# The loads of the Fourier position tables, issued behind the pooling windows instead of behind the values

## The chip, the cores and the metric

The kernel runs on one core of one Trainium2 chip. The metric is the time of one execution on the device, in microseconds (us). Before the change the median of three runs is 1839.31 us (1837.73 to 1840.53).

## What is computed

The reference is a two-layer encoder trunk over 512 positions of 1024 channels, in float32. Each layer adds half a SwiGLU feed-forward (inner width 2816), then a mixer, then half a second SwiGLU. The mixer projects the normalised input once and runs three groups beside each other:

```python
h = rmsnorm(x, mix_norm[l])
p = h @ w_in[l]                       # columns: a 256, f 256, q 512, k 512, v 512
y_pool = pool_mixer(a, pool_w[l], pool_scale[l])          # windows 2, 4, 8, 16, minus the token
y_four = fourier_mixer(f, fourier_w[l])                   # Re(2-D DFT over positions, channels) @ w
y_attn = diff_attention(q, k, v, lam, lam_init, head_norm)  # 4 heads, two softmaxes each
x = x + concatenate([y_pool, y_four, y_attn]) @ w_out[l]
```

The Fourier part along the positions is a product with tables of cosines and sines, which lie in memory (`dft_s`) and are loaded in each layer.

## The kernel before

All products are split into high and low parts: an operand is rounded to a high part on ScalarE (ACT), and the rest becomes the low part on VectorE (DVE), GpSimd (POOL), or through ACT and an accumulating DMA that POOL issues (`split`, L102; `produce`, L171). Three matmuls on TensorE (PE) then make one product (`mm3`, L106). Weights come in tiles of 128 x 1024 through a ring of 7 `st` buffers; SP issues their loads in a fixed sequence (`load`, L159). An operand is converted three ahead of its use (`AHEAD`).

Between these, the tiles of a layer's mixer come from one general pool of 54 buffers (`NG`, L52, `gen`, L77): inputs of the projections, scores, transposed scores, values, tables. PSUM has 8 banks.

The mixer (L605) is written as steps, and the string `ORDER` (L54) names them in the program's order; a scheduler then lays out each engine's instructions, gives out buffers as they come free, and places the waits. Each engine works through its own queue in order. The steps that matter here are:

- `V0`, `V1`, `VE`: the values, and their copy out of PSUM (vh, vl). `GD` loads fw and cs, the tables of the Fourier channels. `TD` (L816) loads the five tables of the positions, `tab`, into five buffers of the general pool, from ACT's queue. `TB` (L821) splits them, much later, for `FD0` and `FD1`.
- `T0` to `T3` transpose the scores of a head (L665): PE writes banks, ACT makes th, DVE tl. `X0` to `X3` weight the values by them (AV, then osq, osh, osl; L677). `Y0` to `Y3` normalise (ss, L274; L688).
- `S20` and the like are scores of a head and a block of queries (L637); `P3`, `A` and `F` are projections (pp, L614): head 3's queries and keys, the pooling input, the Fourier input.
- `GH` (L800) joins the channel tables with the Fourier weights: ACT and DVE split fw and cs, PE makes twelve matmuls, ACT and DVE split the result.
- `AE0`, `AE1` (L740) make the windows of the pooling on DVE (pad, win, m). `PD`, `PL0` and `PL1` (L734, L767) multiply them by the pooling weights: ACT and DVE split m, PE makes PL.
- `W0a` to `W3` are the output projection (wo, L863).

```python
def do_table_loads():
    four["rt"] = [g(w=NT, name="tab") for _ in range(5)]
    for j, t in enumerate(four["rt"]):
        nc.scalar.dma_start(t, dft_s[:, j * NT : (j + 1) * NT])
...
for n in ORDER:
    steps[n]()
```

Loads that SP and ACT issue count on eight semaphores in turn. Each load waits in its engine's queue until the load that had its semaphore before, eight loads earlier in the program, has landed.

Of the kernel before, what the change touches and what calls it, by code (L numbers as in the profile page):

```python
# [36 lines left out]
L = 2  # L37
# [14 lines left out]
NG = 54  # L52
NWARM = 8
ORDER = (  # L54
    "P0 N L P1 E1 P2 E0 S01 S11 S13 E2 V0 S03 S00 S10 S12 S22 S02 S21 T0 V1 GD VE TD T1 X0 S23 S20 Y0 P3 "
    "T2 PD X1 E3 Y1 A GH S30 S32 AE0 AE1 F PL0 X2 S31 S33 PL1 FE0 T3 W0a FE1 Y2 FG0 W1a FG1 TB X3 FD1 FD0 "
    "Y3 W0b W1b W2 W3"
).split()

C_FFN1, C_MIX, C_FFN2, C_FIN = 0, 16, 32, 48  # L60
# [941 lines left out]
```

## Time and profile before

| | us |
|---|---|
| median of three runs | 1839.31 |
| the profiled execution, whole | 1840.45 |
| its span, first to last instruction | 1838.7 |
| TensorE busy in the span | 1773.4 |
| VectorE busy | 1278.8 |
| ScalarE busy | 884.9 |

Times in the views are microseconds from the span's start. A row of the timeline has the start, the duration, the engine, the line of the kernel, the operation and the tiles written and read; in brackets is the idle time of the engine ahead of it and what ended that. `PEld` is the loading of a matmul's stationary operand, and ACTq, SPq and the like are the issuing of DMAs from an engine's queue. The granted clock is TensorE's, as a share of full speed.

### The profile page before, as it was taken

How to read it: one execution, taken by the hardware profiler on the slowest of the kernel's cores; microseconds unless marked ns; L12 is line 12 of the kernel's file. 1: busy time of each engine (PE TensorE's matmuls, PEld its weight loads, DVE VectorE, ACT ScalarE, POOL GpSimd, SP SyncE). 2: the span in 40 equal slices, each digit the busy share in tenths (PEclk: the TensorE clock that was granted, in tenths of full speed). 3: DMA queues.
4: the chain of work that ended last, by engine and by line, in shares of the span. 5: the costliest groups of instructions: out<-in, count | busy, mean ns of one | idle time of the engine just before them, and what ended most of it. 6: DMA issues, size and time to landing. Idle time of an engine off the chain costs nothing.

```text
span 1838.7 us, 28135 instructions
## 1 busy us (share of the span) xinstructions
PE 1773.4 (96%) x11286; PEld 1602.7 (87%) x11286; DVE 1278.8 (70%) x2004; ACT 884.9 (48%) x1223; POOL 204.8 (11%) x242
## 2 busy tenths in 40 slices
PE   8999999999899999999999999999988999999997
PEld 7889989877678989989899899998766899899895
DVE  7765846868679765847887477477776887477474
ACT  7433424468646533424554244244875554244243
POOL 1101001001101101001010010100111110010101
PEclk9999999999899999999999999999998999999998
DMA  7757757545625857857677586665444467586661
GB/s 240 184 149 161 197 133 175 143 124 131 138 67 130 192 160 154 202 130 179 152 169 188 136 195 173 138 169 155 115 118 104 102 158 188 133 200 162 140 158 46
DMA packets 81778, 279.69 MB, mean 152 GB/s; under 512 B 9200, under 2 KB 12784, under 8 KB 81648
## 3 DMA queue, kind: packets, MB, share of 16 engines
q0 software_dynamic: 29376, 106.97, 33.6%
q1 hardware_dynamic: 48528, 166.73, 28.0%
q10 hardware_dynamic: 3744, 4.21, 0.8%
q8 instruction: 88, 1.44, 0.3%
q14 instruction: 42, 0.34, 0.1%
HBM read 258.99 MB, written 2.10 MB: 142 GB/s over the span
## 4 chain that ended last, share of the span: by engine, by line
PE 79%; DVE 6%; ACT 5%; DMA 4%; issue 4%; POOL 1%; SPq 0%; ACTq 0%; DVEq 0%; POOLq 0%
PE dn L107 8%; PE dn L108 8%; PE dn L109 8%; PE qg L462 4%; PE qg L464 4%; PE qg L463 4%; PE qe L463 4%; PE qe L464 4%; PE qe L462 4%; PE qa L464 4%; PE qa L463 4%; PE qa L462 4%; DMA st<-in_gu 4%; PE qb L463 2%; PE qb L464 2%
## 5 line engine op out<-in xcount | busy, mean ns | idle before, releaser
L103 ACT ACTIVATE hi<-st 128x1024 fp32r<-128x1024 f32 (+2 forms) x420 | 432.9, 1035 | 621.4 <-PE dn L108 223.6
L104 DVE TENSOR_TENSOR lo<-st,hi 128x1024 fp32r<-128x1024 f32 (+2 forms) x420 | 500.7, 1194 | 194.5 <-ACT hi L103 193.0
L108 PE MATMUL dn<-al,hi 128*128 128x512 f32 x704 | 274.6, 390 | 0.0
L109 PE MATMUL dn<-ah,lo 128*128 128x512 f32 x704 | 274.2, 389 | 0.0
L107 PE MATMUL dn<-ah,hi 128*128 128x512 f32 x704 | 271.9, 392 | 0.5
L462 PE MATMUL qg<-xh,hi 128*128 128x256 f32 x688 | 196.9, 286 | 6.1 <-ACT hi L103 3.2
L462 PE MATMUL qe<-xh,hi 128*128 128x256 f32 x688 | 196.9, 286 | 4.3 <-DVE nv L328 2.3
L463 PE MATMUL qg<-xh,lo 128*128 128x256 f32 x688 | 196.1, 285 | 0.9 <-DVE lo L104 0.9
L464 PE MATMUL qg<-xl,hi 128*128 128x256 f32 x688 | 196.1, 285 | 0.0
L464 PE MATMUL qe<-xl,hi 128*128 128x256 f32 x688 | 195.6, 284 | 0.1
L463 PE MATMUL qe<-xh,lo 128*128 128x256 f32 x688 | 195.4, 284 | 0.0
L190 POOL DMA_DIRECT2D st<-in_gu x129 | 116.1, 901 | 673.1 <-DVE lo L104 600.3
L600 DVE SCALAR_TENSOR_TENSOR x<-dn,x 128x512 f32<-128x512 f32 x96 | 66.2, 690 | 168.6 <-PE dn L109 168.6
L107 PEld LDWEIGHTS dn<-ah,hi 128*128 128x128 f32 x704 | 131.3, 188 | 31.9 <-ACT ah L103 5.9
L108 PEld LDWEIGHTS dn<-al,hi 128*128 128x128 f32 x704 | 132.2, 188 | 29.0 <-DVE al L104 2.4
L109 PEld LDWEIGHTS dn<-ah,lo 128*128 128x128 f32 x704 | 132.2, 188 | 26.9
L462 PEld LDWEIGHTS qg<-xh,hi 128*128 128x128 f32 x688 | 133.3, 194 | 7.4 <-ACT hi L103 3.4
L462 PEld LDWEIGHTS qe<-xh,hi 128*128 128x128 f32 x688 | 132.4, 192 | 8.1 <-ACT hi L103 4.9
L463 PEld LDWEIGHTS qg<-xh,lo 128*128 128x128 f32 x688 | 133.5, 194 | 1.1 <-DVE lo L104 1.1
L463 PEld LDWEIGHTS qe<-xh,lo 128*128 128x128 f32 x688 | 132.6, 193 | 1.3 <-issue 0.7
L464 PEld LDWEIGHTS qg<-xl,hi 128*128 128x128 f32 x688 | 133.4, 194 | 0.0
L464 PEld LDWEIGHTS qe<-xl,hi 128*128 128x128 f32 x688 | 132.6, 193 | 0.4 <-DVE xl L104 0.3
(274 smaller groups left out, 3923.3 us busy)
## 6 DMA issues: line engine op xcount, KB each, us to landing
st<-in_gu SPq DMA_DIRECT2D x175, 512.0 KB, 4.6
st<-in_gu POOLq DMA_DIRECT2D x172, 512.0 KB, 5.7
st<-in_dn SPq DMA_DIRECT2D x64, 512.0 KB, 4.2
lo<-st POOLq DMA_DIRECT2D x32, 512.0 KB, 5.0
st<-in_dn SPq DMA_DIRECT2D x32, 384.0 KB, 3.2
st<-in_qk SPq DMA_DIRECT2D x16, 512.0 KB, 3.7
st<-in_wo SPq DMA_DIRECT2D x16, 512.0 KB, 3.8
st<-in_wv SPq DMA_DIRECT2D x8, 512.0 KB, 4.9
```

The source lines that it names most:

```text
L103: A.activation(hi, src, AF.Copy)
L104: (lo_eng or V).tensor_tensor(lo, src, f(hi), SUB)
L107: T.matmul(o, lh, rh, start=start, stop=False)
L108: T.matmul(o, lh, rl, start=False, stop=False)
L109: T.matmul(o, ll, rh, start=False, stop=stop)
L190: G.dma_start(t[:, 0:w], then, accum_op=ADD)
L462: T.matmul(o, wh[:, s], xh, start=start and p == 0 and z == 0, stop=False, **k)
L463: T.matmul(o, wl[:, s], xh, start=False, stop=False, **k)
L464: T.matmul(o, wh[:, s], xl, start=False, stop=stop and p == NK - 1 and z == 1, **k)
L600: V.scalar_tensor_tensor(X[m], b, 0.5, X[m], MUL, ADD)
```

## The change

The step `TD` moves in `ORDER`: from behind `VE`, the copy of the values, to behind `AE0` and `AE1`, ahead of the Fourier projection `F`.

```diff
 ORDER = (
-    "P0 N L P1 E1 P2 E0 S01 S11 S13 E2 V0 S03 S00 S10 S12 S22 S02 S21 T0 V1 GD VE TD T1 X0 S23 S20 Y0 P3 "
-    "T2 PD X1 E3 Y1 A GH S30 S32 AE0 AE1 F PL0 X2 S31 S33 PL1 FE0 T3 W0a FE1 Y2 FG0 W1a FG1 TB X3 FD1 FD0 "
-    "Y3 W0b W1b W2 W3"
+    "P0 N L P1 E1 P2 E0 S01 S11 S13 E2 V0 S03 S00 S10 S12 S22 S02 S21 T0 V1 GD VE T1 X0 S23 S20 Y0 P3 "
+    "T2 PD X1 E3 Y1 A GH S30 S32 AE0 AE1 TD F PL0 X2 S31 S33 PL1 FE0 T3 W0a FE1 Y2 FG0 W1a FG1 TB X3 "
+    "FD1 FD0 Y3 W0b W1b W2 W3"
 ).split()
```

Both layers use it. The instructions are the same in number and kind; the scheduler lays some of them out otherwise, on PE, DVE and ACT. POOL and SP keep their sequences. Layer 0 is shown, and layer 1 moves alike. In brackets stand the semaphores that an instruction waits for: those of the engines, and those of loads that SP and ACT issue (DMAHW) or POOL (DMASW).

On ACT, behind the copy of the values (vh), before: the five loads of the tables stand ahead of the conversions of T1 (th).

```order
L728 ACTIVATE vh_4463<-v_4133,ny_3840 128x512
L819 DMA tab_4467<-in_dft_s 128x258 [waits DMAHW5_49]
L819 DMA tab_4468<-in_dft_s 128x258 [waits DMAHW6_49]
L819 DMA tab_4469<-in_dft_s 128x258 [waits DMAHW7_49]
L819 DMA tab_4470<-in_dft_s 128x258 [waits DMAHW0_49,DVE_49]
L819 DMA tab_4471<-in_dft_s 128x258 [waits DMAHW1_49]
L103 ACTIVATE th_4482<-T_440_4477 128x512 [waits PE_49]
```

And now, at the same place:

```order
L728 ACTIVATE vh_4463<-v_4133,ny_3840 128x512
L103 ACTIVATE th_4472<-T_435_4467 128x512 [waits PE_49]
L103 ACTIVATE th_4481<-T_438_4476 128x512 [waits PE_49]
L103 ACTIVATE th_4490<-T_441_4485 128x512 [waits DVE_49,PE_49]
L103 ACTIVATE th_4499<-T_444_4494 128x512 [waits DVE_49,PE_49]
L684 ACTIVATE osq_4516<-AV_447_4503 128x512 [waits PE_49]
```

The five issues and their waits are gone from here; the conversions follow the values at once.

On ACT ahead of the high part of the pooling's m (g from m), before: two conversions of a W1a weight (hi, lo) stand among the exponentials and scalings of head 3's scores (sc).

```order
L657 ACTIVATE sc_4866<-sc_4866,rc_4862 128x512 [waits DVE_49]
L652 ACTIVATE sc_4895,rs_4883<-sc_4895,nb_4882 128x512
L186 ACTIVATE hi_5150<-st_4765 128x1024 [waits PE_49]
L657 ACTIVATE sc_4888<-sc_4888,rc_4884 128x512 [waits DVE_49]
L187 ACTIVATE lo_5151<-hi_5150 128x1024 [waits DMASW1_49,PE_49,Activation_49]
L103 ACTIVATE g_5005<-m_4907 128x512 [waits DVE_49]
```

And now:

```order
L657 ACTIVATE sc_4856<-sc_4856,rc_4852 128x512 [waits DVE_49]
L652 ACTIVATE sc_4885,rs_4873<-sc_4885,nb_4872 128x512 [waits DVE_49]
L186 ACTIVATE hi_4950<-st_4594 128x1024 [waits DMAHW0_49,PE_49]
L657 ACTIVATE sc_4878<-sc_4878,rc_4874 128x512 [waits DVE_49]
L187 ACTIVATE lo_4951<-hi_4950 128x1024 [waits DMASW0_49,PE_49,Activation_49]
L819 DMA tab_4931<-in_dft_s 128x258
L819 DMA tab_4932<-in_dft_s 128x258
L819 DMA tab_4933<-in_dft_s 128x258 [waits DMAHW4_49]
L819 DMA tab_4934<-in_dft_s 128x258 [waits DMAHW5_49]
L819 DMA tab_4935<-in_dft_s 128x258
L103 ACTIVATE g_5005<-m_4897 128x512 [waits DVE_49]
L186 ACTIVATE hi_5150<-st_4755 128x1024 [waits DMAHW1_49,PE_49]
```

The five issues stand ahead of m's high part, and the pair for the second W1a weight, hi_5150, has moved behind it; the pair of the first, hi_4950, stands in its place and used to stand ahead of the exponentials.

On DVE around the channel tables, before: the low part of cs (g from cs) stands behind the pooling's pads and waits for PE.

```order
L104 TENSOR_TENSOR g_4830<-fw_4447,g_4829 128x512 [waits DMAHW2_49,Activation_49,Pool_49]
L746 TENSOR_TENSOR pad_4903<-pp_515_4779,r_3902 128x512 [waits PE_49]
L753 TENSOR_TENSOR win_4908<-pad_4903 128x527 [waits DVE_49]
L753 TENSOR_TENSOR win_4910<-win_4908 128x525 [waits DVE_49]
L746 TENSOR_TENSOR pad_4920<-pp_516_4780,r_3902 128x512 [waits PE_49]
L104 TENSOR_TENSOR g_4832<-cs_4448,g_4831 128x256 [waits PE_49,Activation_49]
L104 TENSOR_TENSOR g_4845<-GH_4837,g_4844 128x512 [waits DVE_49,Activation_49]
```

And now:

```order
L104 TENSOR_TENSOR g_4820<-fw_4447,g_4819 128x512 [waits DMAHW2_49,Activation_49]
L104 TENSOR_TENSOR g_4822<-cs_4448,g_4821 128x256 [waits DMAHW3_49,Activation_49]
L746 TENSOR_TENSOR pad_4893<-pp_510_4769,r_3902 128x512 [waits PE_49]
L753 TENSOR_TENSOR win_4898<-pad_4893 128x527 [waits DVE_49]
L753 TENSOR_TENSOR win_4900<-win_4898 128x525 [waits DVE_49]
L746 TENSOR_TENSOR pad_4910<-pp_511_4770,r_3902 128x512 [waits PE_49]
L104 TENSOR_TENSOR g_4835<-GH_4827,g_4834 128x512 [waits Activation_49]
```

The low part of cs has moved ahead of the pads, behind that of fw, and waits for its load and ACT instead of PE. On PE the twelve GH matmuls stand in one run now; before, eight of them stood behind the first 17 matmuls of `F`. Further on, on DVE, the first window of the second half moves behind the end of m's first half, and the two narrow L764 of the second half move ahead of the low part of m.

## The prediction

> **What bounds the kernel now.** I read the page first. TensorE (PE) is busy for 96% of the span and carries 79% of the chain that ended last, so only time in which PE stands still, or runs at a lower clock, can be won.
>
> ```profile
> span 1838.7 us, 28135 instructions
> PE 1773.4 (96%) x11286; PEld 1602.7 (87%) x11286; DVE 1278.8 (70%) x2004; ACT 884.9 (48%) x1223; POOL 204.8 (11%) x242
> PE 79%; DVE 6%; ACT 5%; DMA 4%; issue 4%; POOL 1%; SPq 0%; ACTq 0%; DVEq 0%; POOLq 0%
> ```
>
> Then the timeline of PE through layer 0's mixer, between the values and the output projection. The columns are start, duration, engine, line and operation; the bracket is idle time before the row and what ended it.
>
> ```profile
> 444.70 0.39 PE L644 MATMUL S<-kh,qs 128*128 128x512 f32 x1
> 448.25 0.50 PE L276 MATMUL ss<-osh,ones 128*128 128x512 f32 x1 [1.16 <-ACT osh L103]
> ...
> 480.14 0.39 PE L109 MATMUL pp<-xh,lo 128*128 128x512 f32 x1
> 481.75 0.39 PE L107 MATMUL GH<-g,g 128*128 128x256 f32 x1 [1.23 <-ACT g L103]
> ...
> 484.15 0.39 PE L107 MATMUL pp<-xh,hi 128*128 128x512 f32 x1
> 487.78 0.39 PE L108 MATMUL pp<-xl,hi 128*128 128x512 f32 x1
> 488.07 0.39 PE L109 MATMUL GH<-g,g 128*128 128x256 f32 x1
> 489.12 0.39 PE L109 MATMUL pp<-xh,lo 128*128 128x512 f32 x1
> 495.94 0.39 PE L109 MATMUL pp<-xh,lo 128*128 128x512 f32 x1
> 499.37 0.80 PE L107 MATMUL PL<-g,g 128*128 128x512 f32 x1 [3.04 <-ACT g L103]
> 502.84 0.80 PE L108 MATMUL PL<-g,g 128*128 128x512 f32 x1 [1.81 <-DVE g L104]
> 508.12 0.63 PE L644 MATMUL S<-kh,qs 128*128 128x512 f32 x1
> ```
>
> Four idle times stand here: 1.16, 1.23, 3.04 and 1.81 us. From 484.15 to 487.78 there are 16 steps of one 512-column matmul: 0.227 us each. The eight GH matmuls from 488.07 to 489.12 take 0.131 us each. Third, the windows view, for the clock.
>
> ```profile
> 440.00:464.70 24.70, 21.91 (x102) 17.28 (x102) 17.32 (x39) 17.77 (x33) 4.53 (x5) 1.00 0.60 149
> 464.70:468.10 3.40, 1.10 (x4) 0.70 (x5) 3.27 (x6) 3.21 (x6) 1.27 (x1) 1.00 0.88 196
> 468.10:471.50 3.40, 3.40 (x10) 2.66 (x9) 2.29 (x4) 3.33 (x6) 0.00 (x0) 0.50 0.46 149
> 498.80:509.00 10.20, 7.81 (x18) 5.70 (x19) 5.45 (x14) 1.75 (x5) 0.85 (x1) 0.50 0.77 190
> 1410.20:1413.60 3.40, 1.54 (x8) 1.01 (x8) 3.30 (x13) 3.18 (x10) 0.38 (x1) 1.00 0.00 0
> 1413.60:1417.00 3.40, 3.40 (x12) 2.99 (x13) 3.40 (x11) 1.25 (x2) 0.00 (x0) 0.50 0.00 0
> ```
>
> After the stretch and its length come PE's busy time, the other engines', the granted clock (after POOL), the DMA share and GB/s. Where PE was busy for 1.10 or 1.54 of 3.4 us, the next 3.4 us ran at clock 0.50; through 440.0 to 464.7, with the 1.16 us idle time in it, the clock stayed 1.00. So a long idle time is paid twice: behind the one at 499.37 the clock was 0.50 for 10.2 us. A halved stretch of busy PE loses 1.7 us.
>
> Last, the timelines of ScalarE (ACT) and VectorE (DVE), for who makes PE wait, with the piece of the chain of waits at 439.21.
>
> ```profile
> 439.21 5.37 DMA st<-in_wo
> ```
>
> ```profile
> 441.41 0.39 ACTq L819 DMA_DIRECT2D tab<-in_dft_s  x1
> 441.47 1.27 ACT L728 ACTIVATE vh<-v,ny 128x512 fp32r<-128x512 f32 x2
> 444.60 0.33 ACTq L819 DMA_DIRECT2D tab<-in_dft_s  x1
> 444.98 2.07 ACT L103 ACTIVATE th<-T 128x512 fp32r<-128x512 f32 x4 [2.24 <-PE AV L109]
> 446.90 0.63 ACT L684 ACTIVATE osq<-AV 128x512 f32<-128x512 f32 x1
> 447.56 0.63 ACT L103 ACTIVATE osh<-osq 128x512 fp32r<-128x512 f32 x1
> ...
> 480.34 1.06 ACT L186 ACTIVATE hi<-st 128x1024 fp32r<-128x1024 f32 x1 [1.73 <-PE pp L108]
> 481.61 1.04 ACT L187 ACTIVATE lo<-hi 128x1024 fp32r<-128x1024 f32 x1
> ```
>
> ```profile
> 487.59 0.43 DVE L104 TENSOR_TENSOR g<-cs,g 128x256 fp32r<-128x256 f32 x1 [4.63 <-PE pp L108]
> 489.47 1.29 DVE L104 TENSOR_TENSOR g<-GH,g 128x512 fp32r<-128x512 f32 x2 [1.45 <-ACT g L103]
> 502.09 0.69 DVE L104 TENSOR_TENSOR g<-m,g 128x512 fp32r<-128x512 f32 x1
> 502.70 0.24 DVE L764 TENSOR_TENSOR m<-m,pad 128x8 f32<-128x8 f32 x2
> ```
>
> The fifth table load stands in ACT's queue and is issued only at 444.60: in the program it waits for the semaphore that the weight load of 439.21 also counts on, and that load landed at 439.21 + 5.37 = 444.58. Behind it stand T1's four conversions, osq and osh. And DVE idles 4.63 us before the low part of cs: its buffer is freed only by a matmul of the Fourier projection F, because the 54 buffers of the general pool are all taken, five of them by the tables.
>
> **The change part by part.** The two layers move alike; layer 1's rows below stand 900.5 us later (1399.87 for 499.37).
>
> *The five issues leave the place behind the values.* ACT's conversions then start behind vh, at 442.74 instead of 444.98. PE's eight score matmuls run from 444.70 without the small gap for a bank, which T1's conversions free, and end at 444.70 + 8 x 0.227 = 446.5. The last AV0 matmul stands one step before 444.70, so osq and osh (0.63 each) are done by about 446.2. So ss goes at 446.5 instead of 448.25: 1.75 us. What is late next is osl on DVE; it follows tl, which follows th, and both move by about 2 us, so ss's second matmul does not wait. Everything up to 480 is a chain behind this and moves along. Bounds: 0, if another wait takes the place; 2.24, ACT's whole idle time.
>
> *Five buffers stay free until the pooling is done.* In the new order the low part of cs is second behind fw's on DVE and waits for its load and ACT alone, and ACT converts cs ahead of the weight of L186. So GH starts behind the pooling projection A, at 480.14 + 0.23 = 480.37 instead of 481.75, and all twelve matmuls go together: 12 x 0.131 = 1.6; then 8 scores, 1.8; then F's 48 matmuls, 10.9: F ends at 494.7 instead of 495.94 + 0.23 = 496.2. That is 1.5 us.
>
> Behind F, PE waits for DVE. ACT does the L186 and L187 pair from 480.34 (1.06 and 1.04, end 482.5), then GH's high part (0.6, as osh): GH's low part starts on DVE at 483.1 instead of 489.47, 6.4 us earlier. From there to the low part of m (502.09) DVE has the same operations as before; the order puts two narrow L764 ahead of it, 0.2. So it starts at 502.09 - 6.4 + 0.2 = 495.9 and ends at 496.6. PE has one PL and three AV matmuls ahead of that wait (0.9, to 495.6), idles 1.0 us instead of 3.04 + 1.81, and does the eleven left in 2.5 us if the clock stays up: the next scores start at 499.1 instead of 508.12, **9.0 us**, the 1.5 included. One idle time of 1.0 us leaves a stretch of 3.4 us busy for 2.4, and 1.16 us did not lower the clock, so I take 1.00; the bounds are no wait at all (1.0 more) and one to two halved stretches (1.7 to 3.4 less).
>
> ```profile
> 1399.87 0.76 PE L107 MATMUL PL<-g,g 128*128 128x512 f32 x1 [3.04 <-ACT g L103]
> 1407.76 0.39 PE L644 MATMUL S<-kh,qs 128*128 128x512 f32 x1
> ```
>
> Layer 1 was halved for less long: 499.1 + 900.5 = 1399.6 instead of 1407.76, **8.2 us**.
>
> *The issues in their new place.* They stand on ACT between the conversion of the first W1a weight and m's high part: 5 x 0.39 = 2.0 us. Two of them still wait for a semaphore in the program, those of the next two wo loads behind that of 439.21; the second of these was issued 30 us earlier.
>
> ```profile
> 461.82 6.94 SPq L165 DMA_DIRECT2D st<-in_wo  x2
> ```
>
> F's first weight is free after 24 of F's 48 matmuls, 5.4 us before F ends; behind that ACT has 1.06, a scaling of about 0.7 and 1.04, then the issues: 4.8 us. So m's high part (0.6) is done about when F ends, and well before the low part that PE waits for anyway. I cost it at nothing; uncovered it would be up to 2.0 a layer. One weight pair moves behind m's high part; it belongs to W1b, the last but two of the projection's steps. SP and POOL keep their order.
>
> *The loads themselves.*
>
> ```profile
> DMA to landing us min/median/max: 4.9/5.7/8.0
> 532.89 1.65 ACT L103 ACTIVATE g<-tab 128x258 fp32r<-128x258 f32 x5
> ```
>
> Issued by about 493 and landed 8.0 later at worst, 501, against a use at 532.9 - 9.0 = 523.9 on the same scale: 23 us of cover.
>
> The Trainium skill's page "DMA: Bandwidth & Descriptors", section "Rules for kernel authors", speaks against the change: to overlap, issue a load early and wait for it late. Its section "Issuing engines are not separate DMA queues" adds that where a load is issued from saves only the issue time. By these the most to be had is those five issues' 2.0 us a layer, about 1836; the rows at 444.60 and 487.59 show two costs of an early issue that these sections leave out, so I do not follow them.
>
> **Sum.** 2 x 1.75 + 9.0 + 8.2 = 20.7 us. The profiled execution took 1840.45 us (span 1838.7 and 1.75 around it), so 1819.75 on its terms; the median of the three runs, 1839.31, stands 1.14 lower, which gives **1818.6**.
>
> **The rivals.**
> - *Half clock stays (0.14).* The wait for m's low part falls into a stretch that PE uses for less than about half, as at 464.70 and 1410.20, and each layer pays one or two halved stretches: 1822 to 1825. For: the stretches at 0.50 begin 3.4 us or multiples of it apart, and where they fall is chance. Against: 1.0 us is below the 1.16 that went free. On this the skill's "TensorE: Matmul & The Clock Gate", Part 1, is milder: half rate after at least one idle window of about 3.4 us. By that rule neither 1.0 nor 3.04 us halves the clock; the row at 498.80 shows that 3.04 did, so the measurement decides.
> - *Only the issue stall goes (0.06).* The pool stays full through other tiles, and cs waits as before: 2 x 1.75, so 1835.8. Against: the new order names no PE release for cs.
> - *Given back at the second FFN (0.06).* PE gets there 10 us earlier, but its first loads do not:
>
> ```profile
> 501.29 2.96 SPq L165 DMA_DIRECT2D st<-in_gu  x2
> ```
>
> These take the buffers of the W1a conversions, the second of which follows F's end and so moves by 1.75 + 1.5; if they bound the next stage, 2 x 3.25: 1832.8. Against: the steps W0b to W3 still lie between.
> - *The tables come late (0.03), slower.* The tables are used by FD0. From a landing of 8 + 23 = 31 us on, each further microsecond delays both layers; from 41 us on the gain is gone, and at 45 us it is 1818.6 + 2 x 14 = 1847. Against: 8.0 at worst so far.
>
> **How the numbers follow.** The forecast has 0.71. Its range: upwards one halved stretch in each layer and a further one (5.1), and A's 1.75 lost twice (3.5): 1827; downwards no wait for m (2.0) and three halved stretches that do not come back, such as those from 468.10 and 1413.60 (5.1): about 1812. That also holds the half-clock rival, together 0.85, and leaves out the rest. A measurement can tell about 0.2% from no change, 3.7 us: faster by more than that are the forecast, the half clock and the gain given back, 0.91; the same, only the stall, 0.06; slower, 0.03.
>
> **What would show it.** ss at the place of 448.25 without idle time before it; GH's twelve matmuls in one run right behind A; no idle time of 4.63 before the low part of cs; one idle time near 1.0 us at PL, with the clock at 1.00 behind it. Wrong: cs still waiting for PE, an idle time above 2 us before PL, ACT idle in front of the moved issues, or PE waiting at the tables' use or at the second FFN's first products.

## The result and the profile after

The changed kernel takes **1822.24 us** (median of 4 runs, 1820.56 to 1823.05), the kernel before 1839.42 (median of 4, 1837.73 to 1840.53): ratio 0.9902, 95% interval 0.989 to 0.9915, faster by 17.2 us. The forecast was 1818.6, with a range of 1812 to 1827. The profiled execution is the fastest of the four.

The head of its page: PE is busy for 9.1 us less than before (1773.4), the span is 19.9 us shorter, so PE also stands still for less.

```profile
span 1818.8 us, 28125 instructions
...
PE 1764.3 (97%) x11286; PEld 1599.2 (88%) x11286; DVE 1280.5 (70%) x2004; ACT 885.3 (49%) x1223; POOL 205.2 (11%) x242
...
PE 81%; DVE 8%; ACT 5%; DMA 3%; issue 2%; SPq 0%; ACTq 0%; POOL 0%; DVEq 0%; POOLq 0%
```

The timeline of PE through layer 0's mixer. Here the mixer begins 0.85 us later than in the trace of before, so the rows are compared by their distance from the first of them, T.

```profile
441.11 0.66 PE L670 MATMUL T<-ident,sc 128*128 128x128 f32 x4 [1.05 <-DVE tl L104]
...
447.37 0.39 PE L276 MATMUL ss<-osh,ones 128*128 128x512 f32 x1
...
466.54 0.51 PE L276 MATMUL ss<-osh,ones 128*128 128x512 f32 x1 [3.17 <-ACT osh L103]
467.89 0.79 PE L277 MATMUL ss<-osl,ones 128*128 128x512 f32 x1 [0.85 <-POOL osl L104]
...
480.74 0.28 PE L107 MATMUL GH<-g,g 128*128 128x256 f32 x1
...
482.05 0.28 PE L109 MATMUL GH<-g,g 128*128 128x256 f32 x1
482.17 0.40 PE L644 MATMUL S<-kh,qs 128*128 128x512 f32 x1
...
496.71 0.50 PE L108 MATMUL PL<-g,g 128*128 128x512 f32 x1 [0.76 <-DVE g L104]
...
499.34 0.39 PE L644 MATMUL S<-kh,qs 128*128 128x512 f32 x1
```

The rows of before that the prediction did not show: T, and the second ss (head 1's) with the idle time ahead of it.

```profile
440.26 0.66 PE L670 MATMUL T<-ident,sc 128*128 128x128 f32 x4 [1.05 <-DVE tl L104]
...
466.13 0.49 PE L276 MATMUL ss<-osh,ones 128*128 128x512 f32 x1 [1.74 <-ACT osh L103]
```

The first ss has no idle time any more and stands at T + 6.26 instead of T + 7.99. GH's twelve matmuls go in one run. At PL one idle time of 0.76 is left of 3.04 + 1.81. But the second ss waits 3.17 instead of 1.74: that is new. The windows view around it (after POOL's busy time: the granted clock, DMA share, GB/s):

```profile
464.50:467.90 3.40, 0.51 (x2) 0.19 (x2) 2.43 (x4) 2.92 (x6) 1.26 (x1) 1.00 0.61 120
467.90:471.30 3.40, 3.40 (x8) 2.72 (x9) 2.55 (x4) 3.17 (x6) 0.00 (x0) 0.50 0.48 154
...
494.00:499.00 5.00, 4.25 (x19) 3.21 (x18) 3.35 (x11) 2.75 (x3) 1.70 (x2) 1.00 1.02 198
505.40:508.80 3.40, 3.40 (x13) 2.88 (x12) 3.21 (x11) 1.24 (x3) 0.00 (x0) 0.51 0.30 117
```

At PL the clock stays 1.00. It is still halved behind the second ss, as before, and once at 505.4.

ACT shows what the second ss waits for: the conversion of the pooling weights (g from pw) stands ahead of osq and osh and waits for its load.

```profile
445.74 0.60 ACT L684 ACTIVATE osq<-AV 128x512 f32<-128x512 f32 x1 [0.20 <-PE AV L109]
...
460.67 0.34 ACTq L736 DMA_DIRECT2D pw<-in_pw  x1
461.13 2.04 ACT L103 ACTIVATE th<-T 128x512 fp32r<-128x512 f32 x4
464.93 0.42 ACT L103 ACTIVATE g<-pw 128x256 fp32r<-128x256 f32 x1 [1.76 <-DMA pw<-in_pw]
465.25 0.58 ACT L684 ACTIVATE osq<-AV 128x512 f32<-128x512 f32 x1
...
491.43 1.64 ACTq L819 DMA_DIRECT2D tab<-in_dft_s  x3
493.12 0.63 ACT L103 ACTIVATE g<-m 128x512 fp32r<-128x512 f32 x1 [1.02 <-DVE sc L662]
```

In ACT's timeline of before the same row waited 0.33:

```profile
461.70 0.37 ACTq L736 DMA_DIRECT2D pw<-in_pw  x1
...
464.52 0.42 ACT L103 ACTIVATE g<-pw 128x256 fp32r<-128x256 f32 x1 [0.33 <-DMA pw<-in_pw]
```

The view of the tile pw has the landing of its two loads of 128 KB, one a layer, in before:

```profile
DMA to landing us min/median/max: 2.7/2.7/2.8
```

And after, with SP's wo load, from SP's timeline, that stands just ahead of the one at 460.67:

```profile
DMA to landing us min/median/max: 4.2/4.4/4.6
```

```profile
460.64 7.00 SPq L165 DMA_DIRECT2D st<-in_wo  x2
```

DVE shows the chain behind the buffers: the low part of cs without a wait, and the low part of m at T + 54.86 instead of T + 61.83, 7.0 us earlier.

```profile
480.42 0.41 DVE L104 TENSOR_TENSOR g<-cs,g 128x256 fp32r<-128x256 f32 x1
...
483.43 1.28 DVE L104 TENSOR_TENSOR g<-GH,g 128x512 fp32r<-128x512 f32 x2
...
495.97 0.69 DVE L104 TENSOR_TENSOR g<-m,g 128x512 fp32r<-128x512 f32 x1
```

### The profile page after: what moved, and what is told of

Same layout as the page of the kernel before. It is cut to its first block, busy times and chain, and to the rows that moved or that the text cites. A ratio compares the mean times of both kernels' runs of the same rounds, so it can differ in the third digit from the quotient of the medians.

```text
span 1818.8 us, 28125 instructions
## 1 busy us (share of the span) xinstructions
PE 1764.3 (97%) x11286; PEld 1599.2 (88%) x11286; DVE 1280.5 (70%) x2004; ACT 885.3 (49%) x1223; POOL 205.2 (11%) x242
## 4 chain that ended last, share of the span: by engine, by line
PE 81%; DVE 8%; ACT 5%; DMA 3%; issue 2%; SPq 0%; ACTq 0%; POOL 0%; DVEq 0%; POOLq 0%
PE dn L107 8%; PE dn L108 8%; PE dn L109 8%; PE qg L462 4%; PE qg L463 4%; PE qg L464 4%; PE qe L464 4%; PE qe L463 4%; PE qe L462 4%; PE qa L464 4%; PE qa L463 4%; PE qa L462 4%; DMA st<-in_gu 2%; PE qb L463 2%; PE qb L464 2%
```

## The experiments

**The theory.** The gain is made by the five buffers, between the second ss and the next scores. The stall of ACT's queue is gone too, but what it cost comes back 18 us later, as a wait for the pooling weights. **Rivals:** the stall carries the gain; the missing 3 us sit at PL or in the clock; the tables' cover matters.

All ratios are to the kernel before, run on the same chip; the chips differ by up to 2 us for the kernel before, so the ratios are compared rather than the medians. The diffs show the parts that matter: the lines that register a new step are left out, a remark behind # gives a step's place in `ORDER`, and the lines of `ORDER` are broken as in the changed kernel.

| kernel | median us | ratio (95% interval) |
|---|---|---|
| changed | 1822.24 | 0.9902 (0.989 to 0.9915) |
| 1 five buffers held, loads late | 1838.79 | 0.9995 (0.9984 to 1.0005) |
| 2 stall alone put back | 1823.48 | 0.9911 (0.9899 to 0.9924) |
| 3 pooling weights loaded early | 1822.2 | 0.9913 (0.99 to 0.9926) |
| 4 the same in the kernel before | 1845.79 | 1.0034 (1.0022 to 1.0046) |
| 5 as 3, map conversions ahead of Y1 | 1833.06 | 0.9958 (0.9944 to 0.9973) |
| 6 map conversions ahead of Y1 alone | 1824.45 | 0.9911 (0.9898 to 0.9924) |
| 7 tables loaded at their use | 1825.49 | 0.9915 (0.9902 to 0.9928) |
| 8 two conversions traded | 1818.15 | 0.9884 (0.9871 to 0.9898) |
| 9 changed, beside 8 | 1821.92 | 0.9911 (0.9897 to 0.9924) |

**1. The buffers alone.** Five buffers are taken where the loads used to stand; the loads stay late.

```diff
+            def do_table_hold():                      # step TH, behind VE
+                four["rt"] = [g(w=NT, name="tab") for _ in range(5)]
+                for t in four["rt"]:
+                    G.memset(t[:, 0:1], 0.0)
             def do_table_loads():
-                four["rt"] = [g(w=NT, name="tab") for _ in range(5)]
                 for j, t in enumerate(four["rt"]):
+                    G.tensor_copy(t[:, 0:1], pm[0][:, 0:1])
                     nc.scalar.dma_start(t, dft_s[:, j * NT : (j + 1) * NT])
```

> The changed kernel, but five buffers of the general pool are taken at the old place of the table loads (a one-column POOL memset in each) and the loads are still issued behind the pooling projection (a one-column POOL copy from the pooled windows ahead of each). So ScalarE has no stall behind the values, and the buffers are taken as before. Theory (the buffers carry the gain): the idle time of about 4.6 us on VectorE ahead of the low part of cs is back, PL waits 3.0 and 1.8 again; of the issue stall's 1.75 us a layer about 1.4 are lost again at the pooling weights, so 1839.4 - 0.7 = 1838.7, between 1835.9 and 1839.5. Rival (the issue stall carries the gain): as the changed kernel, 1822.

Measured: 1838.79, so the theory's number, and the rival is out by 17 us. Its DVE timeline has the idle time ahead of cs again (4.62; the view names no releaser):

```profile
482.21 0.68 DVE L746 TENSOR_TENSOR pad<-pp,r 128x512 f32<-128x512 f32 x1
487.52 0.42 DVE L104 TENSOR_TENSOR g<-cs,g 128x256 fp32r<-128x256 f32 x1 [4.62 <-issue]
```

PE waits at PL in one piece of 5.09 and a rest of 0.21 instead of 3.04 and 1.81. That it is one piece is the experiment's own doing: its five issues wait for copies of m and stand ahead of m's high part on ACT.

```profile
498.21 2.40 ACTq L824 DMA_DIRECT2D tab<-in_dft_s  x5
500.67 0.63 ACT L103 ACTIVATE g<-m 128x512 fp32r<-128x512 f32 x1 [2.88 <-DMA tab<-in_dft_s]
```

The end of the wait is not theirs. It hangs on m's low part, which comes late on DVE behind cs as in the kernel before: PL's second matmul stands at T + 62.39 here and at T + 62.58 there. The stall of ACT behind the values really is gone in this kernel: its first ss stands at T + 6.30 and T + 6.26 in the two layers. What that alone gains stays inside the interval of the ratio, 0.9984 to 1.0005.

**2. The stall alone.** Five loads of 128x16 into tiles of their own, which are not used, at the old place.

```diff
+            def do_small_loads():                     # step TS, behind VE
+                for j, t in enumerate(small):
+                    G.tensor_copy(t[:, 0:1], f(vh[0])[:, 0:1])
+                    nc.scalar.dma_start(t, dft_s[:, j * NT : j * NT + 16])
```

> The changed kernel, plus five loads of 128x16 into tiles of their own at the old place of the table loads (each behind a one-column POOL copy from the values, so that they stand there): ScalarE's queue stalls on the same shared semaphore as before, the five buffers stay free. Theory: ss waits about 1.2 us again and everything behind it is some 1.75 us later, but then the load of the pooling weights is issued ahead of the wo load again and lands in 2.8 instead of 4.2 us, which returns 1.4 to 1.9 a layer: 1822.2 + 2 x (1.75 - 1.65) = 1822.4, between 1821 and 1824. Rival (the stall's price adds up): 1822.2 + 3.5 = 1825.7. Rival (the stall carries the whole gain): 1839.

Measured: 1823.48, inside the theory's 1821 to 1824 and below the 1825.7 of a price that adds up; by its ratio it cannot be told from the changed kernel. The two ss of layer 0:

```profile
451.41 0.50 PE L277 MATMUL ss<-osh,ones 128*128 128x512 f32 x1 [1.16 <-ACT osh L103]
...
469.07 0.50 PE L277 MATMUL ss<-osh,ones 128*128 128x512 f32 x1 [1.51 <-ACT osh L103]
```

The wait of 1.16 is back at the first, and the second waits 1.51 instead of 3.17. Its T stands at 442.62, so the first ss is at T + 8.79, 2.5 us later than in the changed kernel (0.60 us of ACT's idle time there ends with a copy on POOL, which the old stall did not have), and the second at T + 26.45, only 1.0 later. On ACT the conversion of pw has no wait in this layer and 0.62 in the other, and the view of its tile has the shorter landing:

```profile
464.83 0.33 ACTq L737 DMA_DIRECT2D pw<-in_pw  x1
465.28 2.04 ACT L103 ACTIVATE th<-T 128x512 fp32r<-128x512 f32 x4
467.45 0.42 ACT L103 ACTIVATE g<-pw 128x256 fp32r<-128x256 f32 x1
```

```profile
DMA to landing us min/median/max: 2.6/2.8/3.1
```

**3. The pooling weights loaded early.**

```diff
             def do_map_loads():
                 nc.scalar.dma_start(four["raw"][1], dft_c)
+                four["pwt"] = g(w=256, name="pw")
+                nc.scalar.dma_start(four["pwt"], pw[l])
             def do_pool_loads():
-                pwt = g(w=256, name="pw")
-                nc.scalar.dma_start(pwt, pw[l])
+                pwt = four["pwt"]
```

> The changed kernel, with the load of the pooling weights issued behind the load of cs, some 20 us earlier. Theory (the missing 3 us were lost because this load came 0.03 us behind a wo load): ScalarE's idle times of 1.76 and 2.10 us on it go, PE's idle time ahead of ss falls from 3.17 and 3.50 to about the 1.74 and 1.61 of before: 1822.2 - 1.4 - 1.9 = 1818.9, between 1817 and 1820.5. Rival (the loss is at PL, or the clock): within 1 us of 1822.2.

Measured: 1822.2, the rival's number. The theory missed the time, not the place. The wait at the second ss is down to 1.35, but GH, which did not wait in the changed kernel, waits 3.25:

```profile
465.47 0.50 PE L276 MATMUL ss<-osh,ones 128*128 128x512 f32 x1 [1.35 <-ACT osh L103]
...
481.02 0.79 PE L107 MATMUL GH<-g,g 128*128 128x256 f32 x2 [3.25 <-ACT g L103]
```

The order on ACT tells why: with the early load the planner puts a second pair of wo conversions (L186, L187) ahead of the conversions of fw and cs; its first half waits 2.77 for PE, and fw and cs stand behind it.

**4. The same in the kernel before.** The diff of experiment 3, made on the kernel before.

> The kernel before, with the load of the pooling weights issued behind the load of cs. Theory: there it landed in 2.7 to 2.8 us and ScalarE waited 0.33 and 0.20 us for it, so at most 0.5 us to gain: 1839.4 - 0.3 = 1839.1, between 1838 and 1840.5. Rival (the wait for this load cost the same before and after): 3.3 us, so 1836.1.

Measured: 1845.79, 6.0 us above the kernel before on the same chip (1839.75), a miss for both. The same reordering happens there: GH waits 4.42 in each layer instead of 1.23, and PL's second wait is 2.5 instead of 1.8. So 3 and 4 test the planner's new order more than the load.

**5 and 6. The map conversions moved too.** The conversions of fw and cs become a step GC ahead of Y1, in 5 with the early load, in 6 without.

```diff
-    "T2 PD X1 E3 Y1 A GH S30 S32 AE0 AE1 TD F PL0 X2 S31 S33 PL1 FE0 T3 W0a FE1 Y2 FG0 W1a FG1 TB X3 "
+    "T2 PD X1 E3 GC Y1 A GH S30 S32 AE0 AE1 TD F PL0 X2 S31 S33 PL1 FE0 T3 W0a FE1 Y2 FG0 W1a FG1 TB X3 "
+            def do_map_split():
+                fwt, cs = four["raw"]
+                four["maps"] = g(F32R), g(F32R), g(F32R, w=256), g(F32R, w=256)
+                split(fwt, *four["maps"][:2])
+                split(cs, *four["maps"][2:])
             def do_channel_maps():
-                fwt, cs = four["raw"]
-                fwh, fwl, ch, cl = g(F32R), g(F32R), g(F32R, w=256), g(F32R, w=256)
-                split(fwt, fwh, fwl)
-                split(cs, ch, cl)
+                fwh, fwl, ch, cl = four["maps"]
```

> The third kernel again (load of the pooling weights behind that of cs), with the conversions of fw and cs taken out of GH into a step of their own ahead of Y1, so that they no longer stand behind a wo weight pair on ScalarE. Theory (two waits trade places: the early load removed the wait at ss, the planner's new order added 3.25 us at GH): the wait at GH goes, that at ss stays near 1.35 instead of 3.17 and 3.51, so 1822.2 - 1.8 - 2.2 = 1818.2; if the clock also stays up behind ss, as it did in the third kernel, 1.7 less in each layer: between 1814.5 and 1819.5. Rival (the wait at ss costs nothing, since PE waits for the same chain later): 1822.2 within 1 us.

> The changed kernel with the conversions of fw and cs ahead of Y1 alone, the load of the pooling weights where it was. Theory: GH did not wait in the changed kernel, and ss waits for the pooling weights as there: 1822.2, between 1821 and 1823.5. Rival (the place of the conversions is the gain of the fifth kernel): below 1820.

Measured: 1833.06, another miss, and 1824.45, 1.0 above the upper end given for 6, with the ratio that the changed kernel has in its second measurement (0.9911): no gain, as expected. In 5, ss waits 1.35 and GH does not wait; but the first PL matmul, which stands behind F without a wait in the changed kernel, waits 5.49 for m's high part:

```profile
498.37 0.79 PE L107 MATMUL PL<-g,g 128*128 128x512 f32 x1 [5.49 <-ACT g L103]
```

On ACT the second W1a pair (L186, L187) stands ahead of m's high part again, and the five issues of the tables behind it take 3.85 us, most of them uncovered:

```profile
493.78 1.06 ACT L187 ACTIVATE lo<-hi 128x1024 fp32r<-128x1024 f32 x1
493.79 3.85 ACTq L823 DMA_DIRECT2D tab<-in_dft_s  x5
497.69 0.63 ACT L103 ACTIVATE g<-m 128x512 fp32r<-128x512 f32 x1 [2.85 <-issue]
```

So the moved issues are free only while ACT is early enough: here they and the pair are what PE waits for, in both layers (5.49 and 5.36).

**7. The tables at their use.** TD stands directly ahead of TB.

```diff
-    "T2 PD X1 E3 Y1 A GH S30 S32 AE0 AE1 TD F PL0 X2 S31 S33 PL1 FE0 T3 W0a FE1 Y2 FG0 W1a FG1 TB X3 "
+    "T2 PD X1 E3 Y1 A GH S30 S32 AE0 AE1 F PL0 X2 S31 S33 PL1 FE0 T3 W0a FE1 Y2 FG0 W1a FG1 TD TB X3 "
```

> The changed kernel with the five table loads issued directly ahead of their conversions, without any cover. Five issues of 0.33 to 0.44 and a landing of 3.0 to 3.6 us (as in the changed kernel) put the first conversion about 4 us later and the first FP product with it; PE has some two microseconds of other products to do there. Theory (the cover is needed, and the five loads cost nothing only because of it): 2 to 4 us a layer, 1822.2 + 6 = 1828, between 1826 and 1831. Rival (PE has enough other work at that place): 1822.2 within 1 us.

Measured: 1825.49, between the theory and the rival; its ratio, 0.9915, cannot be told from the changed kernel's 0.9902 and 0.9911. The table conversions wait up to 2.68 on ACT, and PE only a few tenths:

```profile
527.64 0.73 ACT L101 ACTIVATE g<-tab 128x258 fp32r<-128x258 f32 x2 [2.68 <-DMA tab<-in_dft_s]
```

In PE's timeline the waits are 0.32 and 0.39 ahead of FQ and 0.17 and 0.15 ahead of the next ss, about 0.5 a layer. The planner moved head 3's AV matmuls ahead of the products of the tables and so hides most of the landing. The theory's 6 us fell.

**8 and 9. Two conversions traded.** The load of the pooling weights stays where it is; its conversion moves ahead of AE1 (step PS), and GC, as in experiment 5, takes its place ahead of osq.

```diff
-    "T2 PD X1 E3 Y1 A GH S30 S32 AE0 AE1 TD F PL0 X2 S31 S33 PL1 FE0 T3 W0a FE1 Y2 FG0 W1a FG1 TB X3 "
+    "T2 PD GC X1 E3 Y1 A GH S30 S32 AE0 PS AE1 TD F PL0 X2 S31 S33 PL1 FE0 T3 W0a FE1 Y2 FG0 W1a FG1 TB X3 "
             def do_pool_loads():
                 nc.scalar.dma_start(pwt, pw[l])
+                four["pwt"] = pwt
+            def do_pool_split():
                 four["pw"] = g(F32R, w=256), g(F32R, w=256)
-                split(pwt, *four["pw"])
+                split(four["pwt"], *four["pw"])
```

> The changed kernel with two conversions traded: the pooling weights are loaded where they were, behind the wo load, but converted ahead of AE1, long before PL needs them; the conversions of fw and cs, whose loads landed some 20 us earlier, take the place ahead of osq. Theory (the missing microseconds sit in ScalarE's wait of 1.76 and 2.10 for the pooling weights ahead of osq and osh): that wait goes, the two conversions take 1.0 instead of 0.4, so PE's idle time ahead of ss falls from 3.17 and 3.51 to about 2.0, and GH does not wait; 1822.2 - 1.2 - 1.5 = 1819.5, between 1816 (if the clock also stays up behind ss) and 1821. Rival (PE waits as long at the next place, as in the third and the fifth kernel): within 1 us of 1822.2, or above.

> The changed kernel itself, run beside the eighth on the same chip: ratio to the kernel before 0.9902, 1822 us where the kernel before takes 1839.4.

Measured: 1818.15 (4 runs, 1817.2 to 1819.26) beside 1821.92 (5 runs, 1818.9 to 1824.36): 3.8 us less, the intervals of the two ratios just touching. ACT in this kernel, with the load as late as ever (landing in 4.1 to 4.6):

```profile
459.35 0.34 ACTq L736 DMA_DIRECT2D pw<-in_pw  x1
459.80 2.03 ACT L103 ACTIVATE th<-T 128x512 fp32r<-128x512 f32 x4
461.71 0.65 ACT L103 ACTIVATE g<-fw 128x512 fp32r<-128x512 f32 x1
462.23 0.43 ACT L103 ACTIVATE g<-cs 128x256 fp32r<-128x256 f32 x1
462.53 0.61 ACT L684 ACTIVATE osq<-AV 128x512 f32<-128x512 f32 x1
```

PE waits 1.81 at the second ss and not at GH:

```profile
463.86 0.50 PE L276 MATMUL ss<-osh,ones 128*128 128x512 f32 x1 [1.81 <-ACT osh L103]
...
477.49 0.28 PE L107 MATMUL GH<-g,g 128*128 128x256 f32 x1
```

This is the fastest version that was run. How much of the 3.8 us is the trade is not settled, since the clock has a share in it. The two profiled executions differ by only 0.7 us in their spans (1816.4 and 1817.1). From T to the next scores the traded kernel is 0.95 and 2.26 us ahead; of the 2.26, about 1.4 lie between the second ss and GH, where its clock was 1.00 in layer 1 against 0.87 in its own layer 0 and 0.88 in the changed kernel. Behind that it loses about 1.6 us in each layer again: from the first wo to FP it takes 21.49 and 21.54, and the changed kernel 19.93 in both.

**The marks side by side.** Microseconds from T to the first ss, to the second, and to the scores behind the pooling, layer 0 / layer 1, from PE's timelines, and pw from issue to landing.

| kernel | first ss | second ss | next scores | pw |
|---|---|---|---|---|
| before | 7.99 / 7.96 | 25.87 / 25.70 | 67.86 / 66.86 | 2.8 / 2.7 |
| predicted | 6.24 / 6.21 | 24.12 / 23.95 | 57.11 / 56.91 | none given |
| changed | 6.26 / 6.26 | 25.43 / 25.77 | 58.23 / 58.59 | 4.2 / 4.6 |
| 1 buffers held | 6.30 / 6.26 | 25.73 / 25.12 | 66.58 / 66.41 | 4.5 / 3.9 |
| 2 stall back | 8.79 / 8.47 | 26.45 / 26.66 | 59.44 / 59.41 | 2.6 / 3.1 |
| 8 traded | 6.29 / 6.31 | 24.11 / 24.12 | 57.02 / 55.63 | 4.1 to 4.6 |
| 9 changed, beside 8 | 6.26 / 6.26 | 25.15 / 25.08 | 57.97 / 57.89 | 3.9 / 3.9 |

## Why the prediction was right, and where it was not

*The sign and the mechanism* held. With the five buffers held and nothing else undone (experiment 1) the time is 1838.79, 16.6 of the 17.2 us up again.

*Five buffers stay free.* From the second ss to the next scores PE takes 32.80 and 32.82 instead of 41.99 and 41.16: 9.19 and 8.34 less, against a forecast of 9.0 and 8.2. The steps inside held as well: GH in one run behind A, no wait at cs, one idle time of 0.76 and 0.75 at PL against 1.0, and the clock at 1.00 there. Less than two thirds of it is idle time: in layer 0 PE stands still for 5.35 us less in this stretch and is busy for 3.84 less, with its mean clock at 0.95 instead of 0.85 (layer 1: 5.37 and 2.97, 0.95 instead of 0.88). So the waits were paid twice there, as the prediction had it.

*The five issues leave the place behind the values* was right at its own place: 1.73 and 1.70 us at the first ss against 1.75. **The step that failed is the sentence behind it: "Everything up to 480 is a chain behind this and moves along."** The second ss should have come 1.75 earlier too; it came 0.44 earlier in layer 0 and 0.07 later in layer 1. So the term of 3.5 us was worth 0.4 (1.3 by the second profile of the changed kernel, experiment 9), and the forecast was 3.6 below the median. The prediction had named this case, as the term's lower bound of 0 and as 3.5 us of its range, but gave no place for it. What the sentence overlooked is that a load lies in that chain, and its landing does not move along. Before, pw was issued 0.12 and 0.21 us ahead of the wo load on SP's queue; after, 0.03 and 0.01 behind it, and it landed 1.4 and 1.9 us later. ACT then stood 1.76 and 2.10 us where it had stood 0.33 and 0.20. Experiment 8 takes that wait out of the chain: its second ss stands at T + 24.11 and 24.12, about where the prediction had it. In experiments 3 and 5, where pw is loaded early, it stands at T + 23.7. That the time of experiment 8, 1818.15, is 0.45 from the forecast is in part luck with the clock, as its paragraph says. Experiment 2 shows the other half: with the stall back, the wait for pw falls to 0 and 0.62 and the second ss is 1.0 and 0.9 us later instead of 2.5 and 2.2.

That the order of the two loads makes the landing longer was not tried by itself; it rests on the cases in the last section.

*Luck.* The profiled execution, 1820.56, came within 0.8 us of the 1819.75 that the forecast gives on its terms, although 3.1 us of the first term were missing. Of the 19.9 us between the two profiled executions 17.9 lie between T and the next scores (9.63 and 8.27); the other 2.0 come from places that the prediction did not sum up. The medians are only 17.2 apart.

*The issues in their new place* cost PE nothing, as forecast, but by less than it seems: the view puts ACT's idle 1.02 us ahead of m's high part down to DVE, whose scaling (L662) ends at 492.58, while the last issue ends at 493.07 and the conversion starts at 493.12. The issues hold it up by about 0.5 us. It is done at 493.75, and F's last matmul starts at 494.66, so PE does not see it. Experiment 5 shows the issues uncovered.

*The tables.* Landing in 3.0 to 3.6 us instead of 8.0 at worst, they had more cover than forecast. The rival of late tables was priced far too high: it let PE pay for each microsecond, and experiment 7, with no cover at all, shows about 0.5 us a layer on PE. On the rule of the Trainium skill's "DMA: Bandwidth & Descriptors", section "Rules for kernel authors", to issue a load early: this case's runs do not bear it out for loads that share a pool, since 17.2 us came from issuing five loads later, and experiment 7 found no cover at all to be nearly enough. The "about 1836" that the prediction gave for the five issues alone is 1835.3 by its own 2.0 us a layer.

*Half clock* came in a small way, behind a stretch in which PE was busy for 1.77 of 3.41 us, slightly more than the rival's half: one halved stretch in layer 0, at 505.4, stretched the products from the first wo to FP from 19.92 to 21.55. Before had the like in layer 1, at 1413.6 (21.54), and after has not (19.92); over the two layers this is a draw. The halved stretch behind the second ss is there before and after.

## What to carry to other kernels

A wait that is taken out moves all that follows only as far as the next thing that does not hang on it: walk down the freed chain and look for loads, their queue's neighbours first. A load that is issued long ahead of its use costs the slot that it holds; look for who waits for that slot. And where a planner sets the order, an experiment that shifts one load tests the planner's new order too: compare the orders before reading the time.

## What the runs showed of the hardware that was not expected

A load of 128 KB took 2.6 to 3.1 us to land where it was issued 0.12 to 0.21 us ahead of a load of 512 KB on another queue (before and experiment 2, two layers each), and 3.9 to 4.6 where it was issued 0.01 to 0.04 behind it (the changed kernel in both of its profiles and experiments 1, 6, 7 and 8, two layers each). So one or two tenths of a microsecond in the order of two issues went with 0.8 us of landing or more. That the order is the cause, and not what else was under way at the time, was not tried by itself.
